# HGRN2 scores in blocks of 64 keys for the levels of 2 to 32 tokens, and a last row of the output by halves of its columns

## The chip, the cores and the metric

The kernel runs on one core of one Trainium2 chip. The metric is device time in microseconds (us), from three executions. All inputs lie in the core's HBM before the start, and the output is written there. The core has TensorE (PE; its weight loads are listed apart as PEld), VectorE (DVE), ScalarE (ACT), GpSimd (POOL) and SyncE (SP), whose queue starts nearly all transfers.

## The reference

One layer over 512 tokens of 2048 features. A projection gives the inputs of two mixers, RWKV-7 (16 heads of 64) and HGRN2 (8 heads of 128 keys by 128 values). Their gated outputs go through one output projection, and the result is normalised:

```python
proj = jnp.einsum('btd,dc->btc', h, w_in[l])
o_rwkv, v_first = _rwkv7_branch(rw, ...)
o_hgrn = _hgrn2_branch(hg, lower_bounds[l], g_norm_w[l])
y = jnp.einsum('btc,cd->btd', jnp.concatenate([o_rwkv, o_hgrn], axis=-1), w_out[l])
h = _layer_norm(ALPHA * h + y, ln_w[l], ln_b[l])
```

In HGRN2 a query of token t sees a key of token s <= t through the product of the forget gates between them, feature by feature:

```python
b = jnp.cumsum(lf_c, axis=1)
att = jnp.einsum('btshd,bshd->btsh', q_c[:, :, None] * decay, k_c)   # decay = exp(b_t - b_s), s <= t
o_intra = jnp.einsum('btsh,bshv->bthv', att, i_c)
```

The layer norm subtracts the row's mean, multiplies by 1/sqrt(var + eps) and by a weight per column, and adds a bias per column.

## The kernel before

**The stream of main products.** Both projections are computed to fp32 precision as three fp32r matmuls (`three`, line 426, the matmul on line 431): high part by high part, high by low, low by high, each 128 weight columns by 512 moving columns. They fill TensorE's time. All other work is written as generators of operations and runs beside them: after each main matmul `Plan.pump` goes through the queues of generators and issues whatever the plan, by the costs written into the operations (`mm`, line 308, has TensorE's), holds to be ready. So the order on every engine comes out of these costs when the kernel is built. An fp32 product that is not fp32r (`mm` on fp32 tiles, line 317) costs TensorE several passes.

**HGRN2 (`hgrn_heads`, line 922).** It runs for two heads at once, four times. Decay between tokens is applied by levels: at level w (line 960: 2, 4, ..., 128) the second half of every block of w tokens has its queries multiplied by the decay of the first half, and the first half has its keys multiplied by the decay of the second. What a level needs are the scores of second-half queries against first-half keys in its blocks. Two levels share a visit to TensorE: the level before is kept as copies (`kept`), so that scores of widths w/2 and w are computed together (lines 987 to 1025).

- A first visit (`blocks32` with n = 48) gives the diagonal and width 1: the keys of 32 tokens are the weights, 32 + 16 queries move.
- At w = 4 and w = 16 (widths 2, 4 and 8, 16): for every block of 32 keys the keys are the weights, and the 16 queries in second halves move. 16 blocks, 2 heads and 2 widths make 64 products.
- At w = 64 (widths 32 and 64): 16 products of 32 keys by 32 queries, and 8 of 64 by 64.

`merge` then copies the wanted scores under a mask (VectorE, `cpred`, line 355) into the tile `near`, [128, 4 blocks, 32]; at width 16 `near` is copied in quarters into the zeroed tile `dg` [128, 4, 128], and the scores of widths 32 and 64 are copied there directly. `hgrn_out` (line 1031) multiplies `dg` with the values.

**The output rows.** The output has 4 rows t of 128 tokens and 4 column blocks d of 512. Blocks 0 to 2 are done first; then, for each t, block 3 over 16 tiles of the contraction (line 1473). `row_out` (line 1378) adds the residual (`stt`, line 349, out of PSUM), takes the statistics (`bn_stats`, line 1389), and with d = 3 calls `finish` (line 1318): aggregate, add eps, the power -1/2 on POOL, then the normalisation. In the rows t < 3 ScalarE scales and shifts a block, and VectorE multiplies by the weight and adds the bias. In the last row, t = 3, the blocks 0 and 1 are multiplied by the weight ahead (`premultiply`), so that VectorE subtracts weight times mean (`less_mean`) and then multiplies by 1/std and adds the bias in one instruction, while ScalarE scales the blocks 2 and 3. Each finished block is written out by SP's queue (line 1353), 256 KB.

Of the kernel before, what the change touches and what calls it, by code (L numbers as in the profile page):

```python
# [15 lines left out]
P = 128  # L16
T = 512
# [7 lines left out]
LEVELS = (1, 2, 4, 8, 16)  # L25
# [209 lines left out]
def mixer_kernel(ctx, tc, head, x_r, w_all, par, up, ln_wb, consts, hmask, out):  # L235
# [266 lines left out]
    cst = cpool.tile([P, 3 * P + 32], F32, tag="cst", name="cst")  # L502
# [3 lines left out]
    eye32 = cst[:, 3 * P :]  # L506
    reset = cpool.tile([P, T], mybir.dt.bfloat16, tag="reset", name="reset")
    ones_r = cpool.tile([P, P], F32R, tag="ones_r", name="ones_r")
    hm = cpool.tile([P, 16 * len(LEVELS)], U8, tag="hm", name="hm")
# [16 lines left out]
    def constants():  # L526
        raw = st("ksq", [P, T])[:, : 16 * len(LEVELS)]
# [394 lines left out]
    def hgrn_heads(SS, h0):  # L922
# [4 lines left out]
        qqs, nrs = ([take(*a) for _ in SS] for a in (("q4", [P, 16, 48]), ("nr", [P, P])))  # L927
        totss = [[take("tot", [P, 256]) for _ in range(2)] for _ in SS]

        nears = [n.rearrange("p (c t) -> p c t", t=32) for n in nrs]  # L930
# [5 lines left out]
        def blocks32(ps, n, k, moving):  # L936
            for b in range(16):
                c, g = b // 4, slice(b % 4 * 32, b % 4 * 32 + 32)
                yield mm(ps[g, c * n : c * n + n], k[:, b * 32 : b * 32 + 32], moving(b))

        def merge(near, m, w, scores):
            yield cpred(near.rearrange("p c (b two w) -> p c b two w", two=2, w=w)[:, :, :, 1],
                        hm[:, m * 16 : m * 16 + 16].rearrange("p (b w) -> p b w", w=w)[
                            :, None].to_broadcast([P, 4, 16 // w, w]),
                        scores.rearrange("p c (b w) -> p c b w", w=w))
# [4 lines left out]
        for pi, k, qq in zip(pss, ks, qqs):  # L950
            yield from blocks32(pi, 48, k, lambda b: qq[:, b])
        for pi, near in zip(pss, nears):
            scores = pi.rearrange("p (c t) -> p c t", t=48)
            yield tt(near, scores[:, :, :32], eye32[:, None, :].to_broadcast([P, 4, 32]))
            yield from merge(near, 0, 1, scores[:, :, 32:])
# [4 lines left out]
        for m, w in enumerate((2, 4, 8, 16, 32, 64, 128)):  # L960
# [19 lines left out]
            if w == 16:  # L980
# [8 lines left out]
            both = ((hw, kept, kept), (w, ks, qs))  # L989
            if w < 64:  # L990
                for v, (w1, k1, q1) in enumerate(both):
                    for i, (q, k) in enumerate(zip(q1, k1)):
                        yield from blocks32(ps[:, 64 * (2 * v + i) : 64 * (2 * v + i) + 64], 16, k,
                                            lambda b: q[:, b * 32 : b * 32 + 32].rearrange(
                                                "p (b two w) -> p b two w", two=2, w=w1)[:, :, 1])
                for v, (w1, k1, q1) in enumerate(both):
                    for i, near in enumerate(nears):
                        pi = ps[:, 64 * (2 * v + i) : 64 * (2 * v + i) + 64]
                        yield from merge(near, m + v, w1, pi.rearrange("p (c t) -> p c t", t=16))
                        if w1 == 16:  # L1000
                            for g in range(4):
                                gs = slice(g * 32, g * 32 + 32)
                                yield copy(dgs[i][gs, :, gs], near[gs])
            else:

                for v, (w1, k1, q1) in enumerate(both):
                    n = P // (2 * w1)
                    for i, (q, k) in enumerate(zip(q1, k1)):
                        pi = ps[:, P * (2 * v + i) : P * (2 * v + i) + P]
                        for b in range(4 * n):  # L1010
                            c, o = b // n, b * 2 * w1
                            g = b % 2 * 64
                            at = (b // 2 if w1 == 64 else c) * w1
                            yield mm(pi[g : g + w1, at : at + w1], k[:, o : o + w1], q[:, o + w1 : o + 2 * w1])
                for v, (w1, k1, q1) in enumerate(both):
                    for i, dg in enumerate(dgs):
                        pi = ps[:, P * (2 * v + i) : P * (2 * v + i) + P]
                        for g in range(2):
                            part = pi[64 * g : 64 * g + w1].rearrange("p (c t) -> p c t", t=w1)
                            if w1 == 64:  # L1020
                                yield copy(dg[:64, g::2, 64:], part)
                            else:
                                yield copy(dg[64 * g : 64 * g + 32, :, 64 * g + 32 : 64 * g + 64], part)
# [3 lines left out]
        drop(*nrs)  # L1027
# [269 lines left out]
    stats = cpool.tile([P, 4, 4, 6], F32, tag="stats", name="stats")  # L1297
# [12 lines left out]
    def premultiply(t, d):  # L1310

        if t == 3 and d < AHEAD:
            k = y_keys(t, d * T, d * T + T)
            yield keyed(tt(ys[t][d], ys[t][d], lnw[0][:, 0, d * T : d * T + T]), k, k)
# [248 lines left out]
```

## Time and profile before

| | |
|---|---|
| three runs | 1066.45, 1066.27, 1065.67 us; median 1066.27 |
| the profiled execution | 1066.34 us; its span, first to last instruction, 1064.5 us |
| TensorE busy | 1050.1 us, 99% of the span, 7418 matmuls |
| weight loads busy | 873.6 us, 82% |
| VectorE, ScalarE, POOL busy | 742.3 (70%), 460.0 (43%), 37.7 us (4%) |
| transfers | 108.46 MB, 102 GB/s over the span |
| mean granted clock of TensorE | 0.997 |

Busy time says how much of the span an engine had something in work; matmuls overlap each other in it, so an engine at 99% need not be at its peak. What ends a stretch is read from the waits and from the chain that ended last. A group by line can be that of a helper (`mm` is line 317, `tt` line 340, `stt` line 349), so the tile's name tells what it is: `mix` is the PSUM tile of the small products, `t` stands for the 512-column tiles (queries, keys, their copies, the tile `dg`), `nr` is `near`.

### The profile page before, as it was taken

What the parts mean: (1) busy time and instruction counts of PE and PEld (TensorE: products, weight loads), DVE (VectorE), ACT (ScalarE), POOL (GpSimd) and SP (SyncE); (2) the same over time, 40 slices, a digit from 0 to 9 for tenths busy, and PEclk for the clock granted to TensorE, in tenths of its full rate; (3) what the DMA queues carried; (4) which work ended last, traced back from release to release, by engine and by line L of the source; (5) the groups of instructions that cost most, each with busy time, mean ns of one, the idle gap of its engine ahead of it and who ended that gap; (6) DMA issues with size and microseconds to landing.
All of it is one profiled execution on the core that took longest, in us unless ns stands there. A gap on an engine that the chain in (4) does not pass through costs nothing.

```text
span 1064.5 us, 18700 instructions
## 1 busy us (share of the span) xinstructions
PE 1050.1 (99%) x7418; PEld 873.6 (82%) x7418; DVE 742.3 (70%) x1616; ACT 460.0 (43%) x916; POOL 37.7 (4%) x81
## 2 busy tenths in 40 slices
PE   9999999999999999999999999999999999999995
PEld 8888888888888888888888888888888888888884
DVE  7466996577679678586996764557987876525556
ACT  6445334454453455355335543545345454323321
POOL 0000000000100000100000001000000011000000
PEclk9999999999999999999999999999999999999998
DMA  8122322232323222232231222323222244545613
GB/s 328 58 91 84 90 89 81 73 91 62 97 85 101 80 80 66 79 98 84 80 122 60 69 73 93 91 79 110 90 79 81 62 149 150 196 124 154 208 59 128
DMA packets 34934, 108.46 MB, mean 102 GB/s; under 512 B 4128, under 2 KB 5664, under 8 KB 34720
## 3 DMA queue, kind: packets, MB, share of 16 engines
q1 hardware_dynamic: 34704, 107.08, 31.8%
q8 instruction: 58, 0.95, 0.4%
q14 instruction: 28, 0.23, 0.1%
q10 hardware_dynamic: 144, 0.20, 0.1%
HBM read 99.92 MB, written 7.34 MB: 101 GB/s over the span
## 4 chain that ended last, share of the span: by engine, by line
PE 99%; DVE 1%; issue 0%; DVEq 0%
PE main L431 73%; PE mix L317 9%; PE mix L431 4%; PE acc L431 4%; PE main L1166 3%; PE mix L321 2%; PE main L317 2%; PE acc L317 1%; PE mix L1116 0%; DVE inv L349 0%; DVE inv L340 0%; DVE stats L1389 0%; DVEq L1559 0%; DVE mv L1331 0%; DVE mv L345 0%
## 5 line engine op out<-in xcount | busy, mean ns | idle before, releaser
L431 PE MATMUL main<-xh,wh 128*128 128x512 f32 x864 | 342.4, 396 | 0.0
L431 PE MATMUL main<-xh,wl 128*128 128x512 f32 x864 | 341.9, 396 | 0.0
L431 PE MATMUL main<-xl,wh 128*128 128x512 f32 x864 | 341.5, 395 | 0.0
L330 ACT ACTIVATE wh<-wr 128x512 fp32r<-128x512 f32 x299 | 186.0, 626 | 172.1 <-PE main L431 125.4
L340 DVE TENSOR_TENSOR wl<-wr,wh 128x512 fp32r<-128x512 f32 x299 | 203.8, 684 | 75.5 <-ACT wh L330 70.6
L431 PEld LDWEIGHTS main<-xh,wl 128*128 128x128 f32 x864 | 162.5, 188 | 32.2
L431 PEld LDWEIGHTS main<-xh,wh 128*128 128x128 f32 x864 | 162.4, 188 | 32.2
L431 PEld LDWEIGHTS main<-xl,wh 128*128 128x128 f32 x864 | 162.5, 188 | 31.8
L431 PE MATMUL main<-wl,xh 128*128 128x512 f32 x256 | 101.2, 395 | 0.0
L431 PE MATMUL main<-wh,xl 128*128 128x512 f32 x256 | 101.1, 395 | 0.0
L431 PE MATMUL main<-wh,xh 128*128 128x512 f32 x256 | 101.0, 395 | 0.0
L330 ACT ACTIVATE zz<-mix 64x64 f32<-64x64 f32 (+1 forms) x103 | 28.1, 273 | 69.5 <-PE mix L317 46.9
L431 PEld LDWEIGHTS main<-wh,xh 128*128 128x128 f32 x256 | 48.1, 188 | 10.2 <-DVE t L349 0.4
L431 PEld LDWEIGHTS main<-wh,xl 128*128 128x128 f32 x256 | 48.1, 188 | 9.5
L431 PEld LDWEIGHTS main<-wl,xh 128*128 128x128 f32 x256 | 48.1, 188 | 9.4
L340 DVE TENSOR_TENSOR inv<-inv 64x30 f32<-64x30 f32 (+14 forms) x120 | 38.6, 322 | 3.1
L340 DVE TENSOR_TENSOR inv<-inv,inv 64x30 f32<-64x30 f32 (+14 forms) x120 | 38.6, 322 | 2.9
L349 DVE SCALAR_TENSOR_TENSOR bd<-mix,pc,bd 64x64 f32<-64x64 f32 x112 | 31.0, 282 | 13.5 <-PE mix L317 12.2
L331 ACT ACTIVATE t<-main,om 128x512 f32<-128x512 f32 x33 | 22.4, 688 | 41.5 <-PE main L431 31.9
L349 DVE SCALAR_TENSOR_TENSOR t<-main,pr,t 128x511 f32<-128x511 f32 x33 | 24.3, 745 | 22.7 <-ACT t L331 22.6
L340 DVE TENSOR_TENSOR t<-t,tot 128x256 f32<-128x256 f32 x96 | 36.9, 417 | 0.2
L331 ACT ACTIVATE t<-main 128x512 f32<-128x512 f32 x32 | 18.7, 596 | 28.2 <-PE main L431 28.1
(239 smaller groups left out, 1364.7 us busy)
## 6 DMA issues: line engine op xcount, KB each, us to landing
wr<-w_all SPq DMA_DIRECT2D x156, 512.0 KB, 3.6
q<-head SPq DMA_DIRECT2D x15, 448.0 KB, 5.4
g<-x_r SPq DMA_DIRECT2D x16, 256.0 KB, 4.0
spill<-g SPq DMA_DIRECT2D x12, 256.0 KB, 3.9
t<-spill SPq DMA_DIRECT2D x12, 256.0 KB, 4.1
out<-q SPq DMA_DIRECT2D x12, 256.0 KB, 2.5
big<-ln_wb SPq DMA_DIRECT2D x1, 2048.0 KB, 8.7
up<-up SPq DMA_DIRECT2D x8, 128.0 KB, 2.8
```

The costliest lines, as they stand in the source:

```text
L317: return Op([("pe", cost, lambda: pe.matmul(o, l, r, start=start, stop=stop, **kw))], [l, r], [o], mode="narrow" if narrow else "main" if ...
L321: return Op([("pe", 0.11, lambda: pe.transpose(o, i, ident))], [i], [o])
L330: return "act", cost, lambda: sc_e.activation(o, i, f, scale=scale)
L331: return "act", cost, lambda: sc_e.activation(o, i, f, scale=scale, bias=bias)
L340: return dve_op([a, b], o, lambda: dve.tensor_tensor(o, a, b, f), base=0.16 if o.shape[0] < P and size(o) == C and o.tensor.name in tags e ...
L349: return dve_op([a, b], o, lambda: dve.scalar_tensor_tensor(o, a, s, b, f1, f2), per=0.00113, base=0.085 if o.shape[0] == P else 0.25 if s ...
L431: pe.matmul(ps, l, r, start=first and i == 0, stop=last and i == 2)
L1166: pe.matmul(pss[a], *ops, start=k == 0 and low == of == 0, stop=k == KT - 1 and low == 1)
```

## The change

**Scores.** The widths 2 to 32 are computed in blocks of 64 keys, with the 32 queries that lie in second halves: 8 blocks, 2 heads and 2 widths make 32 products at w = 4 and at w = 16. At w = 64 the width 32 is 16 products of 64 keys by 32 queries; width 64 stays. `near` is [128, 4, 64], the mask has 32 columns per width and one width more, and the first visit's scores, still in blocks of 32 keys, are spread to both halves of `near` under an identity of period 64. `dg` is zeroed at w = 64, and `near` goes into it in two halves. The planner's cost of a narrow product of 33 to 64 weight columns and up to 32 moving ones is 0.03 us.

**The last row.** Of row 3, block 3, the last four contraction tiles are done in two halves of 256 columns, each in its own PSUM bank. The sum over the first twelve and the residual go into y at once; each half is added, has its statistics taken (five groups of them, not four) and is multiplied by the weight. All four blocks of the row are multiplied by the weight ahead. For the blocks 2 and 3 TensorE forms bias - mean * rstd * weight in PSUM: a product of the identity with the bias, and one of a diagonal, made by ScalarE, with the weight. VectorE then finishes each block with one instruction, block 3 and its output in two halves.

```diff
-LEVELS = (1, 2, 4, 8, 16)
+LEVELS = (1, 2, 4, 8, 16, 32)
...
-            cost = 0.025 if m <= 32 else 0.06 if m <= 64 else 0.16
+            cost = 0.025 if m <= 32 else 0.16 if m > 64 else 0.06 if n > 32 else 0.03
...
+        nears = [take("nr", [P, 4, C]) for _ in SS]
...
+        def blocks(ps, m, k, moving):
+
+            n = size(moving(0))
+            for b in range(T // m):
+                c, g = b * m // P, slice(b * m % P, b * m % P + m)
+                yield mm(ps[g, c * n : c * n + n], k[:, b * m : b * m + m], moving(b))
...
-            if w == 16:
+            if w == 64:
                 yield room(t=2)
...
+            parts = []
+            for m1, w1, k1, q1 in ((m, hw, kept, kept), (m + 1, w, ks, qs)):
+                for i, (q, k) in enumerate(zip(q1, k1)):
+                    pi = ps[:, P * len(parts) : P * len(parts) + P]
+                    parts.append((pi, i, m1, w1))
+                    if w1 < 64:
+                        yield from blocks(pi, C, k, lambda b: q[:, b * C : b * C + C].rearrange(
+                            "p (b two w) -> p b two w", two=2, w=w1)[:, :, 1])
+                        continue
...
+            for pi, i, m1, w1 in parts:
+                if w1 < 64:
+                    yield cpred(later(nears[i], w1), mask(m1, w1),
+                                pi.rearrange("p (c b w) -> p c b w", c=4, w=w1))
+                    continue
...
+    def finish_last(t, pbs, weigh):
...
+        dg = st("ksq", [P, T])[:, :P]
+        yield from spread(t, mv, rs, 5)
+
+        def made():
+            for d in (2, 3):
+                yield mm(pbs[d], dg, columns(t, d)[1], start=False)
+                done.add(f"made{d}")
...
+        def norm():
+            yield small(ts(mv[:, 2:3], mv[:, 0:1], -1.0, None, ALU.mult), k_mv, k_n)
+            yield less_mean(0)
+            yield from weigh()
+            yield small(stt(mv[:, 3:4], mv[:, 0:1], -1.0, rs, ALU.mult, ALU.mult), k_mv + k_r, k_m)
+            yield keyed(Op([("act", 0.25, lambda: sc_e.activation(dg, ident, AF.Copy, scale=mv[:, 3:4]))], [], []),
+                        k_m, [dg.tensor.name])
+            plan.add(scans[0], made())
+            yield less_mean(1)
...
+    LATE = KT - 4
...
+                yield keyed(tt(yc, yc, pc, ALU.add), kc + [pc.tensor.name], kc)
+                yield keyed(Op([("dve", 0.07 + T // 2 * 0.00105,
+                                 lambda: dve.bn_stats(stats[:, t, d + i], yc))], [], []), kc, [f"stat{t}"])
...
+        def biased(pbs):
+            for e in (2, 3):
+                yield mm(pbs[e], ident, columns(t, e)[2], stop=False)
...
+        for i in range(2):
+            c = slice(i * T // 2, i * T // 2 + T // 2)
+            ph = main_ps(banks[::2])[:, : T // 2]
+            for n in range(LATE, KT):
+                k = korder[n]
+                hi, lo = part(q0 + seq.index((3, n)), T)
+                three(ph, gh[k][:, sl], gl[k][:, sl], hi[:, :, c], lo[:, :, c], n == LATE, n == KT - 1)
+            halves.append(ph)
```

**How the instructions move.** TensorE, the first visit at w = 4, between main products (`main<-w..`); `mix` takes the scores, the first two rows are the kept width of the two heads, the next two the new one. Before:

```order
L431 MATMUL main_1293<-wl_1510,xh_77 128x512
L317 MATMUL mix_1540<-t_1093 32x16 x16
L317 MATMUL mix_1540<-t_1295 32x16 x16
L317 MATMUL mix_1540<-t_972,t_1094 32x16 x16
L317 MATMUL mix_1540<-t_1204,t_1296 32x16 x16
L431 MATMUL main_1293<-wh_1509,xl_93 128x512
```

Now:

```order
L431 MATMUL main_1302<-wl_1509,xh_77 128x512
L317 MATMUL mix_1543<-t_1093 64x32 x8
L317 MATMUL mix_1543<-t_1295 64x32 x8
L317 MATMUL mix_1543<-t_972,t_1094 64x32 x8
L317 MATMUL mix_1543<-t_1204,t_1296 64x32 x8
L431 MATMUL main_1302<-wh_1508,xl_93 128x512
```

The place is the same, the products are half as many, with output 64 partitions (weight columns) by 32. The same happens at w = 16. TensorE at w = 64, before:

```order
L317 MATMUL mix_1812<-t_1093 32x32 x8
L317 MATMUL mix_1812<-t_1295 32x32 x8
L317 MATMUL mix_1812<-t_972,t_1094 64x64 x4
L317 MATMUL mix_1812<-t_1204,t_1296 64x64 x4
L431 MATMUL main_1317<-wh_1772,xh_82 128x512
```

Now:

```order
L317 MATMUL mix_1726<-t_1093 64x32 x8
L317 MATMUL mix_1726<-t_1295 64x32 x8
L317 MATMUL mix_1726<-t_972,t_1094 64x64 x4
L317 MATMUL mix_1726<-t_1204,t_1296 64x64 x4
L431 MATMUL main_1325<-wl_1638,xh_81 128x512
```

The count is the same, and the first sixteen have twice the weight columns. VectorE behind the last sum over the contraction, in the last row (`inv` holds its blocks, `big` the weight and the bias, `mv` and `rs` the scalars). Before:

```order
L349 SCALAR_TENSOR_TENSOR inv_9400<-g_10295,mix_10273 128x512
L1389 BN_STATS stats<-inv_9400 128x6
L1331 BN_AGGR mv_10350<-stats 128x2
L345 TENSOR_SCALAR mv_10350<-mv_10350 128x1 x2
L349 SCALAR_TENSOR_TENSOR inv_9399<-big_9232,mv_10350,inv_9399 128x512
L349 SCALAR_TENSOR_TENSOR mv_10350<-mv_10350,rs_10351 128x1
L349 SCALAR_TENSOR_TENSOR inv_9399<-big_9232,mv_10350,inv_9399 128x512
L349 SCALAR_TENSOR_TENSOR inv_9399<-inv_9399,rs_10351,big_9232 128x512
L340 TENSOR_TENSOR inv_9400<-inv_9400,big_9232 128x512
L349 SCALAR_TENSOR_TENSOR inv_9399<-inv_9399,rs_10351,big_9232 128x512
L340 TENSOR_TENSOR inv_9400<-inv_9400,big_9232 128x512 x3
```

Now, from the second half of the columns on (`main` is the PSUM bank of that half, `acc` the two that hold bias and mean):

```order
L340 TENSOR_TENSOR inv_9120<-inv_9120,main_10071 128x256
L1517 BN_STATS stats<-inv_9120 128x6
L1325 BN_AGGR mv_10091<-stats 128x2
L345 TENSOR_SCALAR mv_10091<-mv_10091 128x1 x2
L349 SCALAR_TENSOR_TENSOR inv_9119<-big_8958,mv_10091,inv_9119 128x512
L340 TENSOR_TENSOR inv_9120<-inv_9120,big_8958 128x256
L349 SCALAR_TENSOR_TENSOR mv_10091<-mv_10091,rs_10092 128x1
L349 SCALAR_TENSOR_TENSOR inv_9119<-big_8958,mv_10091,inv_9119 128x512
L349 SCALAR_TENSOR_TENSOR inv_9119<-inv_9119,rs_10092,big_8958 128x512 x2
L349 SCALAR_TENSOR_TENSOR inv_9120<-inv_9120,rs_10092,acc_10089 128x512
L349 SCALAR_TENSOR_TENSOR inv_9120<-inv_9120,rs_10092,acc_10090 128x256 x2
```

Five instructions over 512 columns and five over 256 stand where nine over 512 stood. TensorE at the end, now:

```order
L431 MATMUL main_10071<-wh_9788,xh_9088 128x256
L431 MATMUL main_10071<-wl_9789,xh_9088 128x256
L431 MATMUL main_10071<-wh_9788,xl_9089 128x256
L317 MATMUL acc_10089<-big_8958,cst 128x512
L317 MATMUL acc_10090<-big_8958,cst 128x512
L317 MATMUL acc_10089<-big_8958,ksq_10093 128x512
L317 MATMUL acc_10090<-big_8958,ksq_10093 128x512
```

Before, the stream ended with the main products. Now the bias (`cst`, the identity) and the mean (`ksq`, the diagonal) follow them.

## Rows read from the trace of the kernel before

**Rows 1.** Busy time, share of the span and instructions of each engine, from the page.

```profile
PE 1050.1 (99%) x7418; PEld 873.6 (82%) x7418; DVE 742.3 (70%) x1616; ACT 460.0 (43%) x916; POOL 37.7 (4%) x81
```

**Rows 2.** The page's chain that ended last, shares of the span by engine.

```profile
PE 99%; DVE 1%; issue 0%; DVEq 0%
```

**Rows 3.** Waits of TensorE: line, releaser: us in total, times, longest.

```profile
PE mix L317 <- issue: 2.4, 3, 1.1
```

**Rows 4.** Windows, the eight 16-column visits: us, busy by engine (instructions), clock, DMA.

```profile
169.55:170.75 1.20, 1.20 (x130) 1.17 (x129) 0.00 (x0) 0.00 (x0) 0.00 (x0) 1.00 0.00 0
399.35:401.80 2.45, 1.40 (x129) 1.28 (x128) 0.28 (x1) 0.00 (x0) 0.00 (x0) 1.00 0.62 189
...
sum 12.58, PE 10.22 PEld 9.73 DVE 3.46 ACT 1.26 POOL 0.00; mean PE 1.28 PEld 1.22 DVE 0.43 ACT 0.16 POOL 0.00
```

**Rows 5.** Windows, the first of the four visits at w = 64.

```profile
179.61:180.85 1.24, 1.24 (x49) 1.13 (x49) 0.00 (x0) 0.00 (x0) 0.00 (x0) 1.00 0.88 297
```

**Rows 6.** Windows, the first of four RWKV visits with 64 by 64 products.

```profile
259.70:261.72 2.02, 2.02 (x65) 1.95 (x65) 1.41 (x3) 0.12 (x1) 0.00 (x0) 1.00 0.06 22
```

**Rows 7.** Timeline of weight loads in three visits: start us, us, engine, line, operation, shapes.

```profile
169.54 0.62 PEld L317 LDWEIGHTS mix<-t 128*32 128x32 f32 x63 [0.35 <-issue]
...
179.60 0.59 PEld L317 LDWEIGHTS mix<-t 128*32 128x32 f32 x32 [0.35 <-issue]
...
259.70 1.95 PEld L317 LDWEIGHTS mix<-zz,big 128*64 128x64 f32 x64 [0.37 <-issue]
```

**Rows 8.** Groups by form, narrow products: busy us, mean ns of one, idle before.

```profile
L317 PE MATMUL mix<-t 128*32 128x16 f32 x512 | 5.9, 185 | 0.0
L317 PE MATMUL mix<-t 128*32 128x32 f32 x128 | 2.8, 197 | 0.0
...
L317 PEld LDWEIGHTS mix<-zz,big 128*64 128x64 f32 x256 | 7.8, 138 | 1.3 <-issue 0.7 <-PE main L431 0.4 <-ACT t L331 0.2
L317 PEld LDWEIGHTS mix<-t 128*32 128x32 f32 x640 | 7.5, 110 | 3.2 <-issue 2.0 <-DVE wl L340 0.4 <-PE main L431 0.4
```

**Rows 9.** Timeline of the end, TensorE's last matmul and VectorE.

```profile
1053.15 0.40 PE L431 MATMUL mix<-wh,xl 128*128 128x512 f32 x1
1053.58 0.69 DVE L349 SCALAR_TENSOR_TENSOR inv<-g,mix 128x512 f32<-128x512 f32 x1 [2.39 <-PE mix L431]
1054.30 0.69 DVE L1389 BATCH_NORM_STATS2 stats<-inv 128x6 f32<-128x512 f32 x1
1055.03 0.26 DVE L1331 BATCH_NORM_AGGREGATE mv<-stats 128x2 f32<-128x24 f32 x1
...
1055.58 0.75 DVE L349 SCALAR_TENSOR_TENSOR inv<-big,mv,inv 128x512 f32<-128x512 f32 x1
...
1058.91 1.89 DVE L340 TENSOR_TENSOR inv<-inv,big 128x512 f32<-128x512 f32 x3
```

**Rows 10.** Timeline of TensorE, four transposes between main products.

```profile
900.11 0.39 PE L431 MATMUL main<-wh,xh 128*128 128x512 f32 x1
900.35 0.60 PE L321 MATMUL mix<-cst,t 128*128 128x128 f32 x4
...
901.25 0.40 PE L431 MATMUL main<-wh,xh 128*128 128x512 f32 x1
```

**Rows 11.** Timeline of TensorE, fp32 products of 128 by 128.

```profile
193.62 0.61 PE L317 MATMUL mix<-ia,t 128*128 128x128 f32 x4
194.06 0.39 PE L317 MATMUL mix<-t,t 128*128 128x128 f32 x2
```

**Rows 12.** Groups by form: VectorE on 256 columns, ScalarE on 128.

```profile
L340 DVE TENSOR_TENSOR t<-t,t 128x256 f32<-128x256 f32 x16 | 6.3, 415 | 0.1
...
L330 ACT ACTIVATE t<-mix 128x128 f32<-128x128 f32 x8 | 2.2, 277 | 14.4 <-PE mix L317 14.4
```

**Rows 13.** Windows behind the last matmul.

```profile
1053.50:1058.00 4.50, 0.05 (x1) 0.00 (x0) 4.28 (x10) 1.52 (x2) 0.54 (x1) 0.90 0.00 0
1058.00:1064.50 6.50, 0.00 (x0) 0.00 (x0) 2.79 (x5) 0.00 (x0) 0.00 (x0) 0.50 0.42 161
```

More of the change, by code (lines that the diff above doesn't have):

```diff
@@ L934, in hgrn_heads, with later, mask @@
             yield copy(qq[:, :, 32:], q.rearrange("p (b j two) -> p b j two", b=16, two=2)[:, :, :, 1])
[L936 to L945, printed above, removed]
+        def blocks(ps, m, k, moving):
[3 more added lines that the diff above has]
+                yield mm(ps[g, c * n : c * n + n], k[:, b * m : b * m + m], moving(b))
+        def later(x, w):
+            return x.rearrange("p c (b two w) -> p c b two w", two=2, w=w)[:, :, :, 1]
+        def mask(m, w):
+            return hm[:, m * 32 : m * 32 + 32].rearrange("p (b w) -> p b w", w=w)[:, None].to_broadcast(
+                [P, 4, 32 // w, w])
         yield landed(*ks, *qqs)
@@ L988, in hgrn_heads @@
             ps = take("mix")
[L989 to L1023, printed above, removed]
@@ new lines, in hgrn_heads @@
+            for pi, i, m1, w1 in parts:
[3 more added lines that the diff above has]
+                    continue
+                for g in range(2):
+                    gs = slice(g * 64, g * 64 + 64)
+                    yield copy(dgs[i][gs, :, gs], nears[i][gs])
+                    yield copy(dgs[i][:64, g::2, 64:], pi[gs].rearrange("p (c t) -> p c t", t=64))
@@ L1333, in finish @@
-        yield keyed(rsqrt(rs, mv[:, 1:2]), k_v, k_r)
-        first = [d for d in range(4) if t == 3 and d < AHEAD]
-        rest = [d for d in range(4) if d not in first]
-        if first:
-            yield small(ts(mv[:, 2:3], mv[:, 0:1], -1.0, None, ALU.mult), k_mv, k_n)
-        def less_mean(d):
-            y, w, b, o, k = columns(d)
-            return keyed(stt(y, w, mv[:, 2:3], y, ALU.mult, ALU.add), k + k_n, k)
-        def weighted(d):
-            y, w, b, o, k = columns(d)
-            return keyed(tt(y, y, w), k, k)
@@ L1347, in last @@
-        def last(d):
-            y, w, b, o, k = columns(d)
-            if d in first:
-                yield keyed(stt(y, y, rs, b, ALU.mult, ALU.add), k + k_r, k)
-            else:
-                yield keyed(tt(y, y, b, ALU.add), k, k)
-            nc.sync.dma_start(o, y)
+        k_st, k_mv, k_v, k_n, k_r, k_m = norm_keys(t)
+        yield from spread(t, mv, rs, 4)
         def norm():
-            for d in first:
-                yield less_mean(d)
             ahead = []
-            for d in first + rest:
-                if d in rest:
+            for d in range(5):
+                if d < 4:
+                    y, w, b, o, k = columns(t, d)
@@ L1481, in mixer_kernel @@
             hi, lo = part(q0 + seq.index((3, n)), T)
-            three(ps, gh[k][:, sl], gl[k][:, sl], hi, lo, n == 0, n == KT - 1)
-        row_out(t, 3, ps)
+            three(ps, gh[k][:, sl], gl[k][:, sl], hi, lo, n == 0, n == KT - 1 or t == 3 and n == LATE - 1)
+        if t < 3:
+            row_out(t, 3, ps)
+            continue
+        halves = []
+        row_last(t, 3, ps, halves)
+        for i in range(2):
+            c = slice(i * T // 2, i * T // 2 + T // 2)
+            ph = main_ps(banks[::2])[:, : T // 2]
[4 more added lines that the diff above has]
+            halves.append(ph)
     plan.until(lambda: not any(plan.queues))
```

122 lines of the change are left out of this document (85 added, 37 removed).

## The prediction

> **What bounds the kernel now.** I read the page's first section, then the chain that ended last, then TensorE's waits. TensorE is busy 99% of the span [rows 1], and the chain lies on it for 99% [rows 2]. Inside the stream it waited in three places only, 2.4 us in all, for "issue" in one group of small products [rows 3]. So a microsecond added to or taken from TensorE's stream is one in the time, and the work of VectorE, ScalarE and the queues before the last matmul is covered. After that matmul (start 1053.15, end 1053.55) the chain runs through VectorE until 1060.80 and an output transfer to 1064.5 [rows 9]. The change touches both places. The profiled execution took 1066.34 us, 0.07 above the median 1066.27; the sum is made against it.
>
> **The score visits.** A pair of heads visits TensorE with narrow products four times: once with 48 query columns (not changed), twice with 16, once at w = 64; there are four pairs. An fp32 product appears as two MATMULs and two LDWEIGHTS: 64 products in the order, x128 in the window.
>
> *Before.* A 16-column visit lasts 1.20 us undisturbed; the eight together 12.58, because three hold a stall (one is 2.45 long with the same 128 loads) [rows 4]. A visit at w = 64 takes 1.24, all four alike [rows 5].
>
> *After* (the two pieces of the order). A 16-column visit becomes 32 products of 64 keys by 32 queries, 64 MATMULs; at w = 64, 16 products of 32 by 32 become 16 of 64 by 32. The count halves, but each load is twice as wide, and no row has 64 weight columns with 32 moving ones. So what sets the pitch? Weight loads follow each other on a strip of the array (four strips for 32 keys, two for 64). From [rows 7], taking off the last load: 32 columns on four strips, (0.62 - 0.11)/62 = 8.2 ns a load, 33 ns per strip; 32 columns on two strips, (0.59 - 0.11)/31 = 15.5 ns, 31 per strip; 64 columns on two strips, (1.95 - 0.14)/63 = 28.7 ns, 57.5 per strip. The first has 16 moving columns, the second 32, and the strip's period is the same. That 16 columns do pass faster is in the MATMULs' durations: 185 against 197 ns, so they have no common floor [rows 8]. The load grows from 110 to 138 ns with 32 more columns, 0.87 ns a column, 28 for 32 and 56 for 64 [rows 8], which is the strip's period. I conclude that a strip waits for its weights wherever there are no more moving columns than weight columns, and take 28.7 ns per MATMUL; the other end is 15.5.
>
> Built on the nearest visit, 64 MATMULs of 64 by 64 in 2.02 us [rows 6] = 63 x 0.0287 + 0.21: the new one's last matmul moves 32 columns fewer, 0.03 less at the 12 ns for 16 of [rows 8]: 1.99. Eight: 15.9 against 12.58, **+3.3**. In this the stalls are gone: they are worth 12.58 - 8 x 1.20 = 3.0, and stand only where 128 loads came within 1.2 us; 64 loads over 2 us never stalled [rows 3, 6]. If they stay, +3.0 more. At w = 64: 48 MATMULs at 28.7, 47 x 0.0287 + 0.21 = 1.56 against 1.24; four, **+1.3**.
>
> By the Trainium skill ("TensorE: Matmul & The Clock Gate", section LDWEIGHTS (loading the stationary operand)) a load takes its columns divided by 1.2 in ns: 53 for 64 columns, where the trace has 57.5 per strip. An estimate by that page alone, 26.7 ns per MATMUL, would lower the two terms by 1.4 together; the measured pitch decides here.
>
> **What else moves on TensorE.** The planner's order shifts: counted over the whole order, TensorE has 175 stretches of 128-wide fp32 work between its main products where it had 165, and 37 narrow visits for 36. A stretch costs little beyond its own work: from 900.11 to 901.25 there are three main products (3 x 0.227, the pace of the main stream) and four transposes (4 x 0.11), 0.02 to 0.03 left [rows 10]. Ten stretches 0.3, a narrow visit 0.1: **+0.4**, between 0 and 0.8. The merges (two columns blocks wider each), fewer copies into the zeroed tiles and the later memset lie on VectorE, ScalarE and POOL, which TensorE does not wait for [rows 3]: nothing. The mask's and constants' longer loads go past SP's queue in the head, where the later weights are not yet wanted: nothing; TensorE's waits inside the stream name no transfer [rows 3].
>
> **The last row.** Its last four key tiles are now done in two halves of 256 columns, 24 matmuls for 12. A weight load of 128 columns and its matmul can follow every 0.11 us: four 128-column MATMULs from 193.62 to 194.06, and four last (0.61 - 0.39)/2 = 0.11 each longer than two [rows 11]; 256 columns at the main rate (0.227 for 512) also take 0.11. 24 x 0.112 to 0.12 = 2.7 to 2.9, against 12 x 0.227 = 2.7: **+0.05**, 0 to 0.2.
>
> Before, VectorE ran 1053.58 to 1060.80, 7.22 us [rows 9]. Now the residual sum over the first twelve key tiles and the whole first half (add, statistics, weight: 3 x 0.42 for 256 columns [rows 12], 1.26) stand beside the second half's 1.35 on TensorE. Behind the last matmul, with VectorE's steps from [rows 9, 12]: add 0.45, statistics 0.45, aggregate and two scalars 0.55, less-mean 0.67, weight of the second half 0.35, bias scalar 0.08, less-mean 0.67, two blocks 1.33, a block from PSUM 0.70, two halves 0.38 + 0.42: 6.05. That is **-1.15**. ScalarE's scaling of the last two blocks is replaced by two bias products right behind the last matmul, one ScalarE copy (277 ns for 128x128 [rows 12]) and two mean products. A 128-column fp32 product is 2 x 0.11, so one of 512 is some 0.87 (an estimate). The scalar stands at 2.6 us behind the last matmul, the copy at 3.05, the products at 4.2 and 5.1 with 0.25 of latency; VectorE wants them at 4.6 and 5.35. So they are covered by about 0.3. If not, VectorE's third block waits, and nothing else is queued behind it but the fourth.
>
> The last output is 128 KB instead of 256. Four outputs kept the transfer engines busy 42% of 6.5 us, 0.68 each [rows 13], so half saves up to 0.34, and nothing if its shorter lines (1 KB for 2) move at half the rate. No row has such an output; I take **-0.3**, the larger end, since the last half has nothing left to share the engines with but its twin.
>
> **Sum.** 3.3 + 1.3 + 0.4 + 0.05 - 1.15 - 0.3 = +3.6; 1066.34 + 3.6 = **1070.0**. Its own range is 1069.1 (28 ns as the load's growth has it, -0.4; no turns, -0.4; the full 0.34 at the end) to 1073 (stalls stay).
>
> **Rivals.**
> *Weights are not the limit (faster).* If the pitch is set by the moving columns or by issue, 64 by 32 runs at 15.5 ns as 32 by 32 does. Place: the same twelve visits. A visit is 63 x 0.0155 + 0.18 = 1.16; eight, -3.3 with the stalls; w = 64, 0.50 + 15 x 0.0287 + 0.21 = 1.14, four, -0.4; with the other terms -4.7: 1061.6. For it: half as many instructions, and no row with fewer moving than weight columns at 64. Against: the 31 and 33 ns with 32 and 16 columns. The twelve visits cost 632 p - 13.5 us more than now at a pitch p; with the other terms, -1.0, the sum turns at 23 ns.
> The Trainium skill ("TensorEngine Tiling (Array Packing)", section Instruction Overhead) says that a matmul with one moving column takes as long as one with 60. By that rule the equal periods of 16 and 32 columns would be a floor of the matmul, not the weights; the 185 and 197 ns speak against it here.
> *The stalls stay*: 1073.0. For: three of eight, cause not shown. Against: half the instructions in a longer time.
> *The mean products come late.* TensorE's granted clock was 0.90 over the 4.5 us behind the last matmul and 0.50 (1.2 GHz) later [rows 13]. At 1.2 GHz the two take 1.74 each and VectorE's last block waits 1.6: 1071.6. Against: only some 1.3 us lie between the bias products and the mean products, and the clock fell later than that.
> *The tail saves nothing* because adding halves costs as much as it hides: 1071.4.
>
> **Numbers.** The forecast with vanished stalls 0.58; stalls stay, wholly or in part, 0.12; late mean products or no saving at the end 0.07; weights not the limit 0.16; something between (pitch near 23) 0.07. A run of this kernel tells about 0.2%, 2.1 us, from no change: under 1064.2 is faster, over 1068.5 slower. The forecast, the stalls and the late tail lie above 1068.5, 0.77 together, of which 0.02 goes to same for errors in the small terms; the faster rival gives 0.16; same is that 0.02 and the pitch between, 0.09. The range is 1064.0 to 1073.0: it takes in the pitch between and most of the stalls, and leaves the faster rival out.
>
> **What would show it.** Right: windows over the new 64 by 32 visits near 1.99 us and over w = 64 near 1.56, weight loads some 28.7 ns apart, no "issue" among TensorE's waits, the last VectorE instruction about 6.1 us behind the last matmul of the main stream, and the mean products done before VectorE asks. Wrong: visits near 1.15, loads at 15 ns; or TensorE waiting for VectorE's merges; or a span behind the last main matmul that is not shorter than 11 us.

## The result and the profile after

The changed kernel took 1070.32 us in the median of five runs (1069.81 to 1070.61), the one before 1065.95 on the same chip (1065.59 to 1066.45): a ratio of 1.0043 [1.0031, 1.0054], **slower by 4.4 us**; the forecast was 1070.0. The execution that was profiled took 1069.81 us with a span of 1067.8.

The page of the changed kernel, busy time and the chain that ended last, to be held against [rows 1, 2]:

```profile
PE 1060.5 (99%) x6926; PEld 883.8 (83%) x6926; DVE 749.7 (70%) x1627; ACT 452.9 (42%) x885; POOL 38.7 (4%) x81
...
PE 99%; DVE 1%; DVEq 0%; issue 0%
```

TensorE has 492 instructions fewer and is busy 10 us longer (3.9 of them behind the main products, below): the instructions that went were short, and those that stayed became longer. Its waits (line, releaser: us in total, times, longest), against [rows 3]:

```profile
PE acc L317 <- ACT ksq L1377: 1.5, 1, 1.5
PE mix L1110 <- DVE inv L1108: 1.1, 1, 1.1
```

The first is new and lies behind the last main product: the mean products wait for the diagonal. The second is in the head, at the start. "issue" no longer stands there: the stalls are gone. TensorE's timeline of the first of the eight visits that had 16 query columns, with the main products on both sides:

```profile
162.68 0.39 PE L431 MATMUL main<-wl,xh 128*128 128x512 f32 x1
163.00 1.13 PE L317 MATMUL mix<-t 128*64 128x32 f32 x32
163.95 1.10 PE L317 MATMUL mix<-t,t 128*64 128x32 f32 x32
164.99 0.50 PE L431 MATMUL main<-wh,xl 128*128 128x512 f32 x1
```

From its first product to the next main product it takes 164.99 - 163.00 = 1.99. The window over this visit, with the sum of all eight, each set by such starts, against [rows 4]:

```profile
163.00:164.99 1.99, 1.99 (x66) 1.95 (x65) 0.00 (x0) 0.00 (x0) 0.00 (x0) 1.00 0.03 8
...
sum 15.92, PE 15.92 PEld 15.59 DVE 3.86 ACT 2.77 POOL 0.00; mean PE 1.99 PEld 1.95 DVE 0.48 ACT 0.35 POOL 0.00
```

and over the first of the four at w = 64, with their sum, against [rows 5]:

```profile
179.44:180.99 1.55, 1.55 (x50) 1.48 (x49) 0.00 (x0) 0.00 (x0) 0.00 (x0) 1.00 0.57 92
...
sum 6.20, PE 6.20 PEld 5.93 DVE 0.49 ACT 0.00 POOL 0.00; mean PE 1.55 PEld 1.48 DVE 0.12 ACT 0.00 POOL 0.00
```

Each visit lasts 1.99 and 1.55 us, without exception (66 and 50 instructions are counted for 64 and 48, because the main products on both sides reach into the windows). Eight and four of them come to +3.34 and +1.24. Weight loads of the first product of that visit on the timeline, where 32 records are complete, against [rows 7]:

```profile
163.00 1.01 PEld L317 LDWEIGHTS mix<-t 128*64 128x64 f32 x32 [0.35 <-issue]
```

(1.01 - 0.14)/31 = 28.1 ns a load, 56 ns per strip with two strips.

The end: VectorE behind the last main product, which the timeline of TensorE shows ending at 1057.56 + 0.28 = 1057.84. VectorE's timeline, against [rows 9]:

```profile
1056.45 0.42 DVE L340 TENSOR_TENSOR inv<-inv,main 128x256 f32<-128x256 f32 x1 [0.43 <-PE main L431]
1056.90 0.43 DVE L1517 BATCH_NORM_STATS2 stats<-inv 128x6 f32<-128x256 f32 x1
1057.37 0.42 DVE L340 TENSOR_TENSOR inv<-inv,big 128x256 f32<-128x256 f32 x1
1057.88 0.42 DVE L340 TENSOR_TENSOR inv<-inv,main 128x256 f32<-128x256 f32 x1
...
1058.79 0.29 DVE L1325 BATCH_NORM_AGGREGATE mv<-stats 128x2 f32<-128x30 f32 x1
...
1061.11 1.41 DVE L349 SCALAR_TENSOR_TENSOR inv<-inv,rs,big 128x512 f32<-128x512 f32 x2
1062.43 1.54 DVE L349 SCALAR_TENSOR_TENSOR inv<-inv,rs,acc 128x512 f32<-128x512 f32 x3
```

The first half's add, statistics and weight stand ahead of the second half's add (1057.88), as the order has it. The last instruction ends at 1063.97, 6.13 behind the last main product, where it was 7.25. TensorE there, timeline of the bias and mean products:

```profile
1057.56 0.28 PE L431 MATMUL main<-wh,xl 128*128 128x256 f32 x1
1057.68 1.88 PE L317 MATMUL acc<-big,cst 128*128 128x512 f32 x4
1061.08 1.98 PE L317 MATMUL acc<-big,ksq 128*128 128x512 f32 x4 [1.52 <-ACT ksq L1377]
```

The mean products end at 1063.06; VectorE starts the block that needs the second of them at 1063.10. The outputs, by issue: KB each, median us to landing, and the busy tenths of the 16 transfer engines in 40 slices of a window of 7 us. Before (1057 to 1064 us; [rows 9, 13] have the end before):

```profile
DMA  0000000007999100699930079999999200000000
...
out<-inv SPq DMA_DIRECT2D x4, 256.0 KB, 2.4
```

Now (1061 to 1068 us):

```profile
DMA  0000000002999999999999999941000000000000
...
out<-inv SPq DMA_DIRECT2D x3, 256.0 KB, 2.5
out<-inv SPq DMA_DIRECT2D x2, 128.0 KB, 2.7
```

Before, the engines had gaps between the outputs; now they work without a gap from the first output to the last.

**Where the time went.** I added up the trace from the start of each stretch of TensorE's work to the start of the next, up to the last main product. Before: narrow products 59.71 us, 128-wide fp32 work 84.73, main products 907.88. After: 64.53, 84.44, 904.79 and 2.86 for the 24 halves (which were 12 main products). So narrow +4.82; main with halves -0.23; the 128-wide work -0.29; together +4.3. From the end of the last main product to the end of the span it was 10.99 and is 9.98: -1.0. The difference of the spans is +3.3, as is 4.3 - 1.0; the profiled execution is the fastest of its five, the medians stand 4.4 apart.

### The profile page after: what moved, and what is told of

Its sections match the earlier page's. It is cut to its first block, busy times and chain, and to the rows that moved or that the text cites. A ratio compares the mean times of both kernels' runs of the same rounds, so it can differ in the third digit from the quotient of the medians.

```text
span 1067.8 us, 17717 instructions
## 1 busy us (share of the span) xinstructions
PE 1060.5 (99%) x6926; PEld 883.8 (83%) x6926; DVE 749.7 (70%) x1627; ACT 452.9 (42%) x885; POOL 38.7 (4%) x81
## 4 chain that ended last, share of the span: by engine, by line
PE 99%; DVE 1%; DVEq 0%; issue 0%
PE main L431 73%; PE mix L317 10%; PE acc L431 4%; PE mix L431 4%; PE main L1160 3%; PE mix L321 2%; PE main L317 2%; PE acc L317 1%; PE mix L1110 0%; DVE inv L349 0%; DVE inv L340 0%; DVE stats L1517 0%; DVEq L1631 0%; DVE mv L1325 0%; DVE mv L345 0%
## 5 line engine op out<-in xcount | busy, mean ns | idle before, releaser
L431 PE MATMUL main<-wl,xh 128*128 128x512 f32 (+1 forms) x262 | 102.9, 393 | 0.0
L431 PE MATMUL main<-wh,xl 128*128 128x512 f32 (+1 forms) x262 | 102.9, 393 | 0.0
L431 PE MATMUL main<-wh,xh 128*128 128x512 f32 (+1 forms) x262 | 102.9, 393 | 0.0
L330 ACT ACTIVATE zz<-mix 64x64 f32<-64x64 f32 (+1 forms) x91 | 25.9, 284 | 62.0 <-PE mix L317 39.6
L372 POOL TENSOR_TENSOR sm<-sm,mhalf 128x8 f32<-128x8 f32 x8 | 13.8, 1730 | 469.1 <-DVE sm L346 469.1
```

The source lines that it names most:

```text
L330: return "act", cost, lambda: sc_e.activation(o, i, f, scale=scale)
L372: lambda: pool.tensor_tensor(o, i, mhalf[:, : size(o)], ALU.pow))], [i], [o])
L431: pe.matmul(ps, l, r, start=first and i == 0, stop=last and i == 2)
```

## The experiments

Two halves of the change apart; then what sets the pitch of the new products; then the stalls; then the end. Times in us; "before" is the kernel before, run on the same chip.

### The two halves of the change

**scores_only**: the changed kernel with the last row as it was.

```diff
-        if t == 3:
+        if t == 3 and d < AHEAD:
...
-    def finish_last(t, pbs, weigh):
```

> The changed scores with the last row as before. Theory (a strip waits for its weights, 28.7 ns a MATMUL): the eight 64 by 32 visits take 1.99 us each, 15.9 together against 12.58, the four at w = 64 1.55 against 1.24, no issue stall; +4.6 us of visits and 0 to 0.3 of turns, so 1070.6 to 1071.1 where the kernel before gives 1065.95. Rival (the loss lies in the reordered stream or in the last row, not in the visits): within 1 us of before, 1065 to 1067.

1071.09 against 1066.01, ratio 1.0048 [1.0035, 1.0060]. Eight visits of 1.99, four of 1.55, no "issue", narrow products 64.55 in sum; main and 128-wide work together take 0.1 more than before. The whole loss, and a little more, comes with the scores.

**tail_only**: the kernel before with the changed last row.

```diff
-        if t == 3 and d < AHEAD:
+        if t == 3:
...
+    def finish_last(t, pbs, weigh):
```

> The changed last row with the scores as before. Theory: VectorE ends 1.1 us earlier behind the last main matmul and the last output lands no sooner than before relative to that, so -1.0 us: 1064.7 to 1065.2 where before gives 1065.95; the issue stalls of some 3 us in the 16-column visits stay. Rival (the halves and the queued transfers give it all back): 1065.8 to 1066.3, the last packet as late behind the last main matmul as before.

1065.73 against 1066.01, ratio 0.9998 [0.9989, 1.0007]: less than the -1.0 expected, and no difference that the runs can tell. Its profile says a part of why it is small: VectorE ends 6.12 behind the last main product for 7.25, but the span ends 10.19 behind it for 10.99. Of 1.1 won on VectorE 0.3 is lost again in the outputs. That leaves 0.8 in the trace, of which the medians show 0.3; the rest stays open. The stalls are still there (1.7 of "issue", in two visits), so the new last row does not remove them. Whether the old scores or the order around them make them is not told apart here, since this kernel has both.

### What sets the pitch

**queries_16**: half the moving columns, 64 weight columns as in the change.

```diff
-    "p (b two w) -> p b two w", two=2, w=w1)[:, :, 1])
+    q[:, b * C + 32 : b * C + 48] if w1 == 32 else
+    q[:, b * C : b * C + 32].rearrange("p (b two w) -> p b two w", two=2, w=w1)[:, :, 1])
```

> The changed kernel with 16 of the 32 queries of each product moving, the same 64 weight columns and the same number of products; the scores of the other 16 queries are left out. Theory: the strip still waits for its weights, 28.7 ns a MATMUL; the eight visits stay at 1.97 to 1.99, 1070.1. Rival (the moving columns set the pitch): visits fall towards 1.1 to 1.5, 1063 to 1067.

1071.08, ratio 1.0049 [1.0034, 1.0065]: 1.0 more than expected. Its trace has one wait of 0.7 for ScalarE ahead of 128-wide work that the changed kernel's does not have. Visits of 1.975 and 1.548. The loads of queries_16 on the timeline:

```profile
163.35 1.01 PEld L317 LDWEIGHTS mix<-t 128*64 128x64 f32 x32 [0.35 <-issue]
```

Its products and loads by form (busy us, mean ns of one):

```profile
L317 PE MATMUL mix<-t 128*64 128x16 f32 x384 | 13.3, 210 | 0.0
L317 PEld LDWEIGHTS mix<-t 128*64 128x64 f32 x384 | 12.2, 138 | 2.7 <-issue 2.0
```

The changed kernel's, by form:

```profile
L317 PE MATMUL mix<-t 128*64 128x32 f32 x384 | 13.5, 224 | 0.0
...
L317 PEld LDWEIGHTS mix<-t 128*64 128x64 f32 x384 | 12.2, 138 | 2.8 <-issue 2.1
```

A product is shorter by 14 ns with half the columns, but the loads take the same 1.01 us for 32 and the visit only loses the 0.015 of its last product. Moving columns do not set the pitch here.

**weights_32**: half the weight columns, 32 moving, the same number of products on the same two strips.

```diff
+    c, g = b // 2, b % 2 * 64
+    op = mm(pi[g : g + 32, c * 32 : c * 32 + 32], k[:, b * C : b * C + 32], ...
...
+    for g in (0, 64):
+        gs = slice(g, g + 32)
+        yield cpred(later(nears[i], w1)[gs], mask(m1, w1)[gs], ...
```

> The changed kernel, where each product of width 32 or less loads the keys of the first 32 tokens of a block only (32 weight columns for 64, the same 32 moving columns, the same number of products on the same two strips); the scores of the other 32 keys of each block are left out. Theory: loads follow each other on a strip after 31 ns, 15.5 ns a MATMUL; the eight visits 1.15 us each for 1.99, the four at w = 64 some 1.14 for 1.55; -8.3 us, 1062 where the changed kernel gives 1070.3. Rival (number of products, moving columns or a floor set the pitch): visits stay at 1.99, 1070.

The visits did what the theory said: 1.135 for the eight. At w = 64 I had expected 1.14 and found 1.243; I had left out that such a visit changes from 32-wide to 64-wide loads in the middle; the kernel before has the same loads there and takes the same 1.24 [rows 5]. The narrow products fell by 8.0, to 56.49. **And the time did not move**: 1070.27, ratio 1.0039 [1.0025, 1.0053]. The two merges per width, over 32 partitions each, gave VectorE more instructions (1669 for 1627; 767 us for 750), and TensorE had to wait for it. The page's chain in weights_32, which in the changed kernel lies on TensorE for 99%:

```profile
PE 90%; DVE 5%; DMA 3%; ACT 1%; issue 1%; DVEq 0%; SPq 0%; ACTq 0%
```

TensorE's longest wait in it:

```profile
PE main L431 <- DVE wl L340: 1.9, 2, 1.6
```

Windows of weights_32 ahead of that wait's end and around it (us, then PE, PEld, DVE, ACT, POOL busy, granted clock, DMA share, GB/s):

```profile
866.00:871.00 5.00, 4.71 (x22) 3.50 (x20) 3.66 (x8) 3.52 (x8) 0.00 (x0) 1.00 0.70 244
871.00:878.00 7.00, 5.36 (x17) 4.00 (x16) 5.91 (x11) 4.31 (x11) 0.00 (x0) 0.76 0.43 124
```

TensorE's timeline there, in weights_32:

```profile
869.91 0.39 PE L431 MATMUL main<-xh,wl 128*128 128x512 f32 x1
870.59 0.50 PE L431 MATMUL main<-xh,wh 128*128 128x512 f32 x1 [0.29 <-ACT wh L330]
870.93 0.40 PE L431 MATMUL main<-xl,wh 128*128 128x512 f32 x1
872.96 0.50 PE L431 MATMUL main<-xh,wl 128*128 128x512 f32 x1 [1.64 <-DVE wl L340]
...
874.30 0.63 PE L431 MATMUL main<-xh,wh 128*128 128x512 f32 x1
874.73 0.63 PE L431 MATMUL main<-xl,wh 128*128 128x512 f32 x1
...
877.40 0.39 PE L431 MATMUL main<-wh,xl 128*128 128x512 f32 x1
```

Behind the wait seven main products start 0.43 apart for 0.227, about half the speed (the lower of the two levels, 1.2 for 2.4 GHz), with a granted clock of 0.76 over the 7 us; then the pace is back. From 869.91 to 877.40 there are 15 starts in 7.49 us that take 15 x 0.227 = 3.4 at the usual pace: 4.1 lost, of which 1.9 are the two waits in the brackets. Over the trace, main and 128-wide work take 7.1 and 2.6 more than in the changed kernel. Of the 5.6 outside these 4.1, some 1.4 are four main products ahead of 128-wide work, between 404 and 599 us, and 0.9 are two at 1009 us; the rest was not followed to its places. TensorE's waits inside the stream come to 3.3 for VectorE and 0.3 for ScalarE, where the changed kernel has none. The planner's order is another one too (184 stretches of 128-wide work for 199), and what the order costs is not told apart from what VectorE's longer work costs.

**weights_32b**: the same with one merge per width, over 32 partitions, so that VectorE has the changed kernel's count again, and the order its 199 stretches.

```diff
-    for g in (0, 64):
-        gs = slice(g, g + 32)
+    for gs in (slice(0, 32),):
```

> As weights_32 (32 weight columns for 64, everything else of the products kept), but with one merge per width as in the changed kernel, over 32 partitions only, so that VectorE has no more instructions than there; the scores of the other keys are left out. Theory: weights_32 had its visits at 1.14 and lost the 8 us again because VectorE's doubled merges made TensorE wait once, near 870 us; without them no wait over 1 us in the stream and the time 8 us under the changed kernel: 1062 to 1063. Rival (shorter visits are given back in the stream whatever VectorE does): 1069 to 1071 again.

1061.84 against 1066.23, ratio 0.9961 [0.9947, 0.9974]: 8.5 less than the changed kernel's median (on another chip; by the two ratios to the kernel before 8.7, by the two profiled spans 7.4). Its visits are as short as those of weights_32, VectorE has its 1627 instructions, and TensorE waits nowhere inside the stream. Loads on the timeline of weights_32b:

```profile
163.36 0.59 PEld L317 LDWEIGHTS mix<-t 128*32 128x32 f32 x32 [0.35 <-issue]
```

A visit's window in weights_32b:

```profile
163.37:164.51 1.14, 1.14 (x66) 1.10 (x65) 0.00 (x0) 0.00 (x0) 0.00 (x0) 1.00 0.07 14
```

(0.59 - 0.11)/31 = 15.5 ns a load where the change has 28.1, at the same count, strips and moving columns. The pitch is the weights'. What halving them gives per visit, 0.85, times eight, and 0.31 times four, is 8.0, and the median shows 8.5.

### The stalls

**split_visits**: the kernel before, each of its eight visits cut in two with other work of TensorE between.

```diff
+    if v:
+        yield lambda: plan.mode == "main"
+        yield landed(*qs, *ks, *kept)
+    ps = take("mix")
```

> The kernel before, with each 16-column visit cut into two, one width each, with at least one main product between. Theory (a stall comes where 256 TensorE instructions are taken within 1.2 us, and half of that is safe): no issue stall in sixteen visits of some 0.62 us; they cost 0.82 each with their turns, 13.1, for eight of 1.40 and 2 to 3 us of stalls, 13.5 to 14.2: 1064.9 to 1066. Rival (the stalls belong to places of the stream and not to the density): two or three stalls of 0.7 to 1.3 us remain, 1067 to 1069.

1067.68 against 1066.23, ratio 1.0013 [1.0004, 1.0022]: slower, where I expected faster. The stalls did nearly go: 15 of the 16 short visits last 0.666 us, one 1.108, and of the 2.4 for "issue" [rows 3] one wait is left among TensorE's waits in split_visits:

```profile
PE mix L317 <- issue: 0.2, 1, 0.2
```

The narrow products lose 1.2 in sum, but the main products take 2.3 more. Of these, 0.9 lie in one place at 872 us where TensorE waits 0.7 for ScalarE; the other 1.4 are 0.17 for each of the eight added visits. So fewer instructions in a row stall less, and coming and going costs more than the 0.1 that I put on a narrow visit. The stalls that went and what the added visits cost nearly cancel (two short visits are 1.33 for 1.20, 1.1 in eight, and 1.4 in main products, against some 2.5 of stalls); what the profiled execution is slower by is mostly that one wait, and whether it comes of the split is not shown. Why three of eight visits stalled and the other five did not, and at which place the supply of instructions fails, stays open.

### The end

**early_output**: tail_only, with block 0 finished and sent off before the second half's weight and block 1's mean.

```diff
+    y, w, b, o, k = columns(t, 0)
+    yield keyed(stt(y, y, rs, b, ALU.mult, ALU.add), k + k_r, k)
+    nc.sync.dma_start(o, y)
     yield from weigh()
```

> The changed last row with the scores as before, and block 0 finished and written before the weight of the second half and the mean of block 1. Theory (the five transfers of the last row run back to back, so the first one's start sets the end): the first output 1.0 us earlier, the last packet some 0.4 us earlier behind the last main matmul, 0.4 under tail_only: 0.7 under before. Rival (the last instruction and a fixed latency set the end): the last packet as in tail_only, no change against it.

1065.58 against 1066.23, ratio 0.9997 [0.9988, 1.0006]. The last packet came 8.42 behind the last main product, as in tail_only (8.44), though SP issued the first transfer 3.10 behind that product (1056.28 - 1053.18) instead of 4.04 (1057.71 - 1053.67). VectorE ended 6.29 behind that product for 6.12. When the first transfer starts does not set the end.

**whole_block**: tail_only, with block 3 finished and written in one piece.

```diff
-    for c in (slice(0, T),) if d < 3 else (slice(0, T // 2), slice(T // 2, T)):
+    for c in (slice(0, T),):
```

> The changed last row with the scores as before, and block 3 finished and written whole, not in halves. Theory (halving the last output gains nothing behind queued transfers and costs an issue on SP): within 0.2 us of tail_only, the last packet no later behind the last main matmul. Rival (the halves bring 0.3 us): 0.3 slower than tail_only.

1065.22 against 1066.23, ratio 0.9993 [0.9984, 1.0002]. The last packet comes at 8.16 and the span ends at 9.75 behind the last main product, where tail_only has 8.44 and 10.19. SP's queue in tail_only:

```profile
1057.71 2.64 SPq L1399 DMA_DIRECT2D out<-inv  x5
```

and in whole_block:

```profile
1057.31 2.33 SPq L1399 DMA_DIRECT2D out<-inv  x4
```

One issue less on SP, 0.3 us, and one VectorE instruction less (6.00 for 6.12). I had expected no more than 0.2 between the two. The changed kernel and three other traces with the halved output end 9.97 to 10.00 behind the last main product, so halving the last output cost 0.2 to 0.4 where I had credited it with 0.3.

**whole_again**: the same kernel once more, beside the next.

> The kernel of whole_block once more, as the measure for weigh_pool on the same chip and to narrow its ratio to the kernel before. Theory (VectorE's end 1.2 us earlier behind the last main matmul, the main stream the same): 0.8 to 1.0 us under before, 1065.2 where before gives 1066.1. Rival (no gain that can be told): within 0.3 us of before.

1065.00 against 1065.82, ratio 0.9996 [0.9987, 1.0005].

**weigh_pool**: whole_block, with the second half multiplied by the weight on POOL.

```diff
+    yield keyed(pool_tt(yc, yc, w, ALU.mult) if i else tt(yc, yc, w), kc, kc)
```

> whole_block with the weight of the last row's second half multiplied by POOL behind its power, not by VectorE. Theory (the chain behind the last main matmul is VectorE's sum of steps): 0.35 us off VectorE's chain, the mean products 0.3 earlier too, so VectorE ends near 5.7 us behind the last main matmul for 6.0 and the time is 0.3 under whole_again. Rival (POOL's product, some 0.8 us, comes late or slows VectorE beside it): VectorE's last block waits or its steps stretch, no change or slower.

1065.12 against 1065.82, ratio 0.9996 [0.9987, 1.0005]. VectorE ended 6.27 behind the last main product, later than the 6.01 of whole_again although it has one instruction of 0.42 less. The timelines of VectorE and POOL in weigh_pool:

```profile
1056.45 0.68 DVE L349 SCALAR_TENSOR_TENSOR mv<-mv,rs 128x1 f32<-128x1 f32 x1
...
1056.28 0.84 POOL L365 TENSOR_TENSOR inv<-inv,big 128x256 f32<-128x256 f32 x1
```

The scalar of one column takes 0.68 beside POOL's product and ends where that one ends (1057.13 and 1057.12); in whole_block it takes 0.15. The rival that POOL's work comes back as VectorE's time held.

In medians the whole block is 1.0 and 0.8 faster than the kernel before. Both comparisons point the same way, but in each the interval holds 1: no version with the whole computation was shown to beat the kernel before.

## Why the prediction was right, step by step

- **The score visits** (+3.3 and +1.3): measured +3.34 and +1.24, and +4.82 for all narrow products, start to start, one narrow visit more among them. The pitch was taken from 64 by 64 products as 28.7 ns and is 28.1. The reason given, that a strip waits for its weights where it has no more moving than weight columns, was argued from three rows that differed in more than one thing; queries_16 and weights_32b changed one thing each in the products, and showed it. The difference of 185 and 197 ns was no sure ground against a floor, since the ends of matmuls are modelled in the trace; the starts of queries_16 show it, with visits of 1.975 us for 1.988. The page's rule on loads in the Trainium skill ("TensorE: Matmul & The Clock Gate", section LDWEIGHTS (loading the stationary operand)) gives 53 ns for 64 columns; the strip's period is 56 here, so the rule holds to 3 ns. For 32 columns it would give 27 (an estimate by that rule), where the strips show 31 and 33.
- **The stalls** (-3.0, in the +3.3): gone, as taken. That half the instructions in a longer time do not stall came out, but it was argued from where the three stalls stood, without a cause; split_visits shows that the number in a row matters, not why.
- **Turns** (+0.4, 0 to 0.8): not found. TensorE has 199 stretches of 128-wide work for 187, by a count on the traces, and main work (halves included) and 128-wide work together take 0.5 less, not more. A mean pace of the 3876 main products that differs by 0.1 ns makes 0.4 already (233.5 and 233.4 here), so a term this small can't be read from one execution. For narrow visits the price was too low, not too high: 0.17 for 0.1 in split_visits. The change adds only one such visit.
- **The last row on TensorE** (+0.05, 0 to 0.2): 24 halves took 2.86, 0.119 each, against 12 x 0.227 = 2.72: +0.14, inside the range.
- **VectorE's end** (-1.15): 6.13 behind the last main product for 7.25, -1.12; tail_only 6.12; the sum of steps was 6.05.
- **The mean products** were to be ready 0.3 ahead of VectorE. ScalarE's copy took 0.40 us where I had put 0.28. The first is ready 0.23 ahead (1062.20 for 1062.43), the second ends at 1063.06, and VectorE takes it up at 1063.10: nothing is left of its margin, and no wait came of it, since VectorE's last three blocks of 512 columns start 0.66 apart and the next one 0.67 behind them. The granted clock of the 4.5 us behind the last main product is 1.00 here, where it was 0.90 with TensorE idle [rows 13]:

```profile
1057.80:1062.30 4.50, 2.98 (x8) 1.12 (x7) 4.29 (x11) 0.40 (x1) 0.54 (x1) 1.00 0.00 0
```

- **The last output of 128 KB** (-0.3): this step failed. From VectorE's end to the span's end it took 10.99 - 7.25 = 3.74 before, 9.98 - 6.13 = 3.85 after and 4.07 in tail_only: +0.1 to +0.3. I gave the last half nothing left to share the engines with but its twin. The two DMA rows above show otherwise: with VectorE faster, the outputs follow each other without a gap, and the last half waits behind them. Its bytes were not the trouble: counted in the changed kernel's trace, the packets of 1 KB took 51 ns in the mean, those of 2 KB 90. 128 KB landed in 2.7 us, 256 KB in 2.5, and SP had one issue more to make; whole_block, which takes this step back, ends 0.4 earlier than tail_only. What sets the end now, VectorE or the transfers, stays open: early_output only rules out the start of the first transfer.

Between the profiled executions the forecast's +3.6 stands against +3.3: narrow products 0.2 more than forecast (4.8 for 4.6), TensorE's other work 1.0 less (-0.5 for +0.45), the end 0.4 worse (-1.0 for -1.45). The small terms were wrong by up to their own size and cancelled; direction and size rest on the visits and on VectorE's end. The median's +4.4 is more because the profiled run before lies 0.4 above its median, and the one after 0.5 below. That the forecast, 1070.0, comes within 0.3 of the median is in part luck: the errors of the terms and this scatter run against each other.

**The rivals.** *Weights are not the limit*, 0.16, would have been 1061.6: weights_32b is what that looks like, 1061.84, with loads 15.5 ns apart, and it needs half the weight columns. The rule of the Trainium skill ("TensorEngine Tiling (Array Packing)", section Instruction Overhead) that products of one to some 60 moving columns take the same isn't what runs here: with 16 columns for 32 the main product behind a visit starts 13 ns sooner, and the records say 210 ns for 224. *The stalls stay* fell with the wait rows above. *The mean products come late* fell with VectorE's even steps, and its ground with the granted clock of 1.00. *The tail saves nothing* held in part: tail_only's median is 0.3 under that of before, which the runs can't tell from nothing, although VectorE is done 1.1 sooner.

## What to carry to other kernels

For small fp32 products on column strips, count weight columns per strip, some 0.9 ns each here, and not instructions: half as many products with loads twice as wide load the same columns through two strips instead of four, and took 1.99 us for 1.20. A wider moving side was free up to the width of the weights (16 and 32 columns here with 64 of weights). A saving on a full engine is worth its time only while its suppliers hold: weights_32 won 8 us on TensorE and lost them again in a stream where VectorE had 17 us more to do. Cut a last output in two only if the row of a shorter transfer shows that it lands sooner, and the transfer engines are free when it comes.

## What the runs showed that was not expected

- One wait of 1.64 us of TensorE was followed by seven main products at half the pace (0.43 us for 0.227) and a granted clock of 0.76 over 7 us. A wait of 1.52 us before the mean products, with the bias products ahead of it, was not: the clock over that stretch stayed at 1.00, in the 2.0 us of work that were left. What makes the difference is not shown.
- A scalar instruction of VectorE took 0.68 us for 0.15 while POOL multiplied 256 columns, and ended with that product.
- Outputs of 128 KB took no less time to land than those of 256 KB (2.7 and 2.5 us), although their packets took little more than half the time: they stood behind other outputs.
- Eight more visits to narrow products cost 0.17 us each in main products, and 0.13 each in longer visits: about as much as the stalls that they avoid.
